# Feed-forward down projection: the short chunk of K moved from first to last, its first column half joined to the last seven-product passes

## The chip, the cores and the metric

The kernel runs on one core of one Trainium2 chip, in one launch. The metric is device time in microseconds (us): a median of three runs. The engines are named as the profile names them: PE (TensorE) multiplies, DVE (VectorE) and ACT (ScalarE) work elementwise, POOL (GpSimd) and SP (SyncE) mostly issue transfers.

## What is computed

The reference is a two-layer encoder on 256 positions with 2048 channels, all in 32-bit floats. Each layer has a mixer (attention with pooling in layer 0, an mLSTM in layer 1) and then a gated MLP. The change touches the MLP alone:

```python
def conv_ffn(x, w_up, conv_w, conv_b, w_down):
    u = x @ w_up
    up = jnp.pad(u, ((0, 0), (1, 1), (0, 0)))
    c = conv_w.astype(u.dtype)
    u = c[0] * up[:, :-2] + c[1] * up[:, 1:-1] + c[2] * up[:, 2:] + conv_b.astype(u.dtype)
    gate, val = jnp.split(u, 2, axis=-1)
    return (jax.nn.silu(gate) * val) @ w_down
```

`w_up` is 2048 x 11264 and `w_down` 5632 x 2048. The layer's output is the residual `x` plus this; it feeds the next RMS norm, or, after layer 1, is the result.

## The kernel before, in words

**Split weights.** Every weight is streamed in chunks of 128 x 1024 floats. `Stream.load` (L105) has SP load a chunk into one of 7 buffers `w`; `Stream.split` (L126) has ACT round it to a high part (L137) and DVE subtract that to get the low part (L138), both into one of 4 buffers `hl`. A product then takes three matmuls: high by high, high by low, low by high. With four `hl` buffers, the split of a chunk can only begin once PE is done with the chunk four before it. The number in a name such as `hl382` is the chunk's place in the whole stream.

**The MLP.** `ffn_layer` works through a list of steps that `_ffn_plan` writes. An `up` step (L1110) makes one 128-wide tile of the 5632 hidden channels: 64 matmuls over 4 weight chunks, then a copy by ACT (L441), adds by DVE (L442, L1114), the convolution (ACT L1119 to L1121, DVE L1122 and L1123), the SiLU gate (L1127, L1128) and the split into the tile `g` (L1129, L1130). There are 44 of them. The down projection sums over these 44 tiles; they are taken in chunks of K, `FCH = [4, 8, 8, 8, 8, 8]`, and its work is woven in behind the `up` steps.

**Seven products in place of eight.** For a pair of K tiles and one half of the columns (two blocks of 512), the plain way takes eight 128 x 128 x 512 products. The kernel takes seven, in two kinds of pass: A makes four (PSUM tiles 4, 6, 5, 3) and B three (0, 1, 2). A step such as `A1` is a pass of kind A on column half 1. Within a pass, steps of one unit handle two pairs: 24 matmuls over 4 weight chunks for A, 18 over 3 for B. A needs sums of the `g` tiles (`combine`, L1132: tiles `sf`, then `s3`, `s1`) and sums of weights. The latter are made by transfers into DRAM far ahead (`premix`, L478: the tiles `m`), or, for every other pair, by a load with an accumulating transfer from POOL (`sum`, L123) and two adds by DVE on the next chunk (L133, L134).

**Draining.** The PSUM pool `ps` has four tiles. When a pass ends, `drain` (L1187, adds at L1199) moves its three or four tiles into `acc` and `x`, one DVE add each. After the last pass of a column half, `total` (L1209) does the eight adds (L1216) that combine the products into the four quarters of `x` in that half. PE executes in the order of the code; DVE, ACT, POOL and SP stand in an order that a scheduler sets.

**The end of the list before.** The last chunk of K has half of its pairs taken with seven products on column half 1 only (`A1+`, `B1+`); everything else of it goes the plain way. Passes of chunk 4 run as `A0 A1 A1+ B0 B1 B1+`. Behind the last `up` step stand two units of B1, the plain block 0 in part (`down_two`, L1266), the unit B1+, the rest of the plain blocks 0 and 1, and then half of the K tiles of blocks 2 and 3 (`down`, L1250). In layer 1 the very last block is `down_end` (L1222), which finishes in three pieces. In layer 0, `Norm.add` (L315) starts on each finished block: squares on ACT, transposes on PE (`xt`, L326) and the split into `xx` (ACT L338, DVE L341), which the mLSTM's first matmuls (`mv`) read.

Of the kernel before, what the change touches and what calls it, by code (L numbers as in the profile page):

```python
# [9 lines left out]
F32 = mybir.dt.float32  # L10
# [6 lines left out]
P = 128  # L17
# [14 lines left out]
FT = DFF // P  # L32
FCH = [4, 8, 8, 8, 8, 8]
CH = 8
BOTH = ((0, 1, 2, 3, 4), (0, 1, 2, 3, 4))
LAST = (4, 4)

PASSES = (
    ("A1 B1 A0 B0", "A1 B1 A0 B0", "A1 B1 A0 B0", "A1 B1 A0 B0", "A0 A1 A1+ B0 B1 B1+"),
    ("A1 B1 A0 B0", "A1 B1 A0 B0", "A1 B1 A0 B0", "A1 B1 A0 B0", "A0 A1 A1+ B0 B1 B1+"),  # L40
)
# [178 lines left out]
def trunk(ctx: ExitStack, tc: tile.TileContext, gx, xT, xn, call, catt, cml, weights, mixes, out):  # L220
# [869 lines left out]
    def ffn_layer(layer, norm, nxt):  # L1090
        with ExitStack() as es:
# [7 lines left out]
            combos, pss, quads, seen, twos = {}, {}, {}, set(), []  # L1099
# [109 lines left out]
            def total(h):  # L1209
# [5 lines left out]
                for n, (to, op, e) in enumerate(steps):  # L1215
                    tc.keep_in_program_order(op(to, to, e))  # L1216
# [33 lines left out]
            def down(c, b):  # L1250
                gt, last = gts[c], c == len(FCH) - 1
                kts = list(range(_direct(layer, c, b), FCH[c]))
# [8 lines left out]
                if last and nxt is None:  # L1261
                    nc.sync.dma_start(out[:, :, b * 512 : b * 512 + 512], x[:, :, b * 512 : b * 512 + 512])
                elif last:
                    nxt.add(b)

            def down_two(c, second):  # L1266

                gt, n = gts[c], FCH[c]
                if not second:
                    twos.extend(mmp.tile([P, 2, 512], F32, tag="mm", name=f"dn{layer}_{c}_{b}") for b in range(2))  # L1270
                parts = [(ps, kts) for kts in (range(n - 2), range(n - 2, n)) for ps in twos]
                for ps, kts in parts[1:] if second else parts[:1]:
                    mov_part(ps, lambda k: gt[:, k], list(kts), kts[0] == 0, kts[-1] == n - 1)
                if not second:
                    return
                wv.until(lambda: ("A", 0) not in seen or ("total", 0) in pss)
                for b, ps in enumerate(twos):
                    residual(ps, b)
                    if nxt is None:
                        nc.sync.dma_start(out[:, :, b * 512 : b * 512 + 512], x[:, :, b * 512 : b * 512 + 512])  # L1280
                    else:
                        nxt.add(b)
# [3 lines left out]
            for kind, c, i, *j in _ffn_plan(layer):  # L1286
                if kind == "up":
# [4 lines left out]
                    if layer == 0 and (c, i) == (len(FCH) - 2, 5):  # L1292
                        premix(2, 25.0, 25.0, 0)
                elif kind == "down":
                    down(c, i)
                elif kind == "two":
                    down_two(c, i)
# [96 lines left out]
def _halves(layer, c):  # L1394

    return () if c == len(FCH) - 1 else (0, 1) if c in BOTH[layer] else (1,)


def _pairs(layer, c):

    return (LAST[layer] if c == len(FCH) - 1 else FCH[c]) // 2


def _direct(layer, c, b):

    return LAST[layer] if c == len(FCH) - 1 and b >= NB // 2 else 0


def _ffn_plan(layer):

    slots, late, units = [[] for _ in range(FT)], [], []
    at = 1
    for c in range(len(FCH) - 1):
        at = max(at + (c == 0) * FCH[0], sum(FCH[: c + 1]))
        step = len(_halves(layer, c))
        for pas in PASSES[layer][c].split():  # L1420
# [191 lines left out]
```

## Time and profile before

| what | before |
|---|---|
| median of 3 runs | 2147.94 us (2147.16 to 2148.05) |
| span of the profiled execution | 2145.3 us, so 2.6 us of the median lie around it |
| busy: PE, DVE, ACT, POOL | 100%, 83%, 67%, 13% of the span |
| DMA | 606.66 MB, mean 283 GB/s |
| last `up` of layer 0, of layer 1 (start) | 905.85 us, 2085.44 us |

A row of a timeline or group gives the start, the busy time, the engine, the line, the operation, what is written and read, and how often; in brackets or behind a bar stands how long the engine was idle before it and what ended that. Busy matmuls overlap: the time that a run of them takes is read from the start of one row to the start of the next.

### The profile page before, as it was taken

The page shows a single profiled execution, that of the slowest core. Times are in us where ns is not written, and L with a number is a line of the kernel's source. Part 1 is how long each engine was busy: PE and PEld are TensorE (multiplying, and loading weights), DVE is VectorE, ACT ScalarE, POOL GpSimd, SP SyncE. Part 2 cuts the span into 40 slices and gives each one's busy share as a digit, 9 for nine tenths or more (in the row PEclk, how much of TensorE's full clock was granted, in tenths as well). Part 3 has the DMA queues.
Part 4 walks back from the last instruction along what each step waited for, and adds up shares of the span by engine and source line. Part 5 has one row for each costly group of instructions (what it writes and reads, how often), then busy time and mean ns, then how long its engine had stood idle before and what let it go on. Part 6 is the DMA issues. An engine that isn't in the chain of part 4 may idle for free.

```text
span 2145.3 us, 32359 instructions
## 1 busy us (share of the span) xinstructions
PE 2139.5 (100%) x11364; PEld 1834.6 (86%) x11364; DVE 1784.1 (83%) x2524; ACT 1444.6 (67%) x2199; POOL 287.6 (13%) x366
## 2 busy tenths in 40 slices
PE   9999999999999999999999999999999999999999
PEld 7888888888888888889888888888888888888887
DVE  7786678889988899898878786567888899889988
ACT  6665577777777767766556564557776777777774
POOL 0022112111111111111111111111111111100000
PEclk9999999999999999999999999999999999999999
DMA  9678889899999999998889798988999999888875
GB/s 333 210 213 256 262 248 317 275 327 329 318 331 320 321 300 306 307 296 237 276 276 299 232 308 236 280 242 247 313 291 333 337 311 317 288 259 266 255 249 189
DMA packets 181543, 606.66 MB, mean 283 GB/s; under 512 B 23707, under 2 KB 26563, under 8 KB 181379
## 3 DMA queue, kind: packets, MB, share of 16 engines
q1 hardware_dynamic: 133952, 478.60, 62.4%
q0 software_dynamic: 28384, 70.54, 19.4%
q10 hardware_dynamic: 19042, 55.45, 7.8%
q8 instruction: 89, 1.46, 0.3%
q14 instruction: 76, 0.61, 0.1%
HBM read 602.35 MB, written 104.90 MB: 330 GB/s over the span
## 4 chain that ended last, share of the span: by engine, by line
PE 97%; DVE 2%; issue 1%; DMA 0%; ACT 0%; ACTq 0%; DVEq 0%
PE up L275 45%; PE pp L275 16%; PE op L275 8%; PE mq L275 4%; PE mk L275 4%; PE mo L275 3%; PE mv L275 3%; PE qproj L275 3%; PE dn L275 3%; PE mp L275 1%; PE kproj L275 1%; PE vproj L275 1%; DVE hl L138 1%; PE pool L275 1%; PE av L275 1%
## 5 line engine op out<-in xcount | busy, mean ns | idle before, releaser
L138 DVE TENSOR_TENSOR hl<-w,hl 128x1024 fp32r<-128x1024 f32 (+1 forms) x869 | 1048.0, 1217 | 179.1 <-ACT hl L137 172.1
L137 ACT CAST hl<-w 128x1024 fp32r<-128x1024 f32 (+1 forms) x868 | 891.2, 1046 | 384.8 <-PE up L275 118.3
L275 PE MATMUL up<-xx,hl 128*128 128x512 f32 (+1 forms) x5632 | 993.6, 337 | 0.0
L275 PEld LDWEIGHTS up<-xx,hl 128*128 128x128 f32 x5632 | 867.0, 188 | 130.0
L491 POOL DMA_DIRECT2D m<-m x184 | 147.4, 816 | 942.9 <-PE up L275 414.0
L275 PE MATMUL pp<-hl,s 128*128 128x512 f32 x912 | 226.5, 390 | 0.4
L275 PEld LDWEIGHTS pp<-hl,s 128*128 128x128 f32 x912 | 168.1, 188 | 34.4 <-DVE hl L138 1.6
L275 PE MATMUL pp<-hl,g 128*128 128x512 f32 x684 | 173.9, 390 | 0.0
L275 PEld LDWEIGHTS pp<-hl,g 128*128 128x128 f32 x684 | 125.8, 188 | 24.4
L441 ACT COPY tb_up<-up 128x512 f32<-128x512 f32 x88 | 51.6, 587 | 116.5 <-PE up L275 116.5
L1122 DVE TENSOR_TENSOR y<-y,z 128x510 f32<-128x510 f32 x88 | 60.8, 690 | 63.2 <-ACT y L1121 62.7
L1121 ACT ACTIVATE y<-tb_up,conv 128x256 f32<-128x256 f32 x176 | 103.7, 589 | 0.0
L491 POOL DMA_DIRECT2D m<-in_dn x80 | 69.2, 864 | 247.1 <-PE up L275 59.4
L275 PE MATMUL mk<-xx,hl 128*128 128x512 f32 (+1 forms) x512 | 93.0, 338 | 0.0
L275 PE MATMUL mq<-xx,hl 128*128 128x512 f32 (+1 forms) x512 | 92.0, 337 | 0.0
L442 DVE TENSOR_TENSOR tb_up<-up,tb_up 128x512 f32<-128x512 f32 x88 | 60.9, 692 | 36.9 <-ACT tb_up L441 36.5
L275 PE MATMUL op<-hl,cat 128*128 128x512 f32 x384 | 91.5, 393 | 0.0
L1119 ACT ACTIVATE z<-tb_up,conv 128x256 f32<-128x256 f32 x176 | 88.2, 501 | 3.9 <-DVE tb_up L1114 2.0
L275 PE MATMUL op<-hl,mcat 128*128 128x512 f32 x384 | 89.7, 392 | 0.0
L275 PEld LDWEIGHTS mq<-xx,hl 128*128 128x128 f32 x512 | 79.2, 188 | 11.6
L275 PEld LDWEIGHTS mk<-xx,hl 128*128 128x128 f32 x512 | 79.3, 188 | 11.4
L1120 ACT ACTIVATE z<-tb_up,conv 128x256 f32<-128x256 f32 x176 | 87.4, 496 | 0.0
(256 smaller groups left out, 2178.8 us busy)
## 6 DMA issues: line engine op xcount, KB each, us to landing
w<-in_up SPq DMA_DIRECT2D x352, 512.0 KB, 6.6
w<-in_dn SPq DMA_DIRECT2D x174, 512.0 KB, 6.0
w<-in_m_in SPq DMA_DIRECT2D x118, 512.0 KB, 6.0
w<-m SPq DMA_DIRECT2D x98, 512.0 KB, 5.7
m<-in_dn ACTq DMA_DIRECT2D x160, 256.0 KB, 5.8
m<-m POOLq DMA_DIRECT2D x184, 128.0 KB, 6.0
w<-in_a_in SPq DMA_DIRECT2D x45, 512.0 KB, 5.5
m<-in_dn POOLq DMA_DIRECT2D x80, 256.0 KB, 7.2
```

Of the source, the lines that this page charges most:

```text
L137: (self.nc.vector.tensor_copy if i + c == 0 else self.nc.scalar.copy)(hl[:, 0, c : c + n], w[:, c : c + n])
L138: low = self.nc.vector.tensor_sub(hl[:, 1, c : c + n], w[:, c : c + n], hl[:, 0, c : c + n].bitcast(F32))
L275: last_mm[0] = pe.matmul(out_, lhsT, rhs, start=start, stop=stop, skip_group_check=True)
L441: a.copy(tb, ps[:, :, 1, :])
L442: v.tensor_add(tb, ps[:, :, 0, :], tb)
L491: paced(eng.dma_start(to[p : p + P // 2], src[p : p + P // 2], **kw))
L1119: a.activation(z[:, 0, j, :], u[:, j, :], AF.Copy, scale=cw(tl, 0))
L1120: a.activation(z[:, 1, j, :], u[:, j, :], AF.Copy, scale=cw(tl, 2))
L1121: a.activation(y[:, j, :], u[:, j, :], AF.Identity, scale=cw(tl, 1), bias=cw(tl, 3))
L1122: v.tensor_add(y[:, :, 1:S], y[:, :, 1:S], z[:, 0, :, 0 : S - 1])
```

## The change

`FCH` becomes `[8, 8, 8, 8, 8, 4]`: the short chunk is the last. All five full chunks take seven products on both halves, and of the last chunk column half 0 joins the last A0 and B0 passes (`A0+`, `B0+`); only blocks 2 and 3 of it go the plain way, four K tiles each. The last passes run as `A1 B1 A0 A0+ B0 B0+`. Since a pass begins when its chunk of `g` is there, six units now stand behind the last `up` step and the one B1 unit after it. `down_two` is gone; `finished` stores a block or hands it to the norm, for blocks 0 and 1 once `total(0)` is through.

```diff
-FCH = [4, 8, 8, 8, 8, 8]
+FCH = [8, 8, 8, 8, 8, 4]
...
-    ("A1 B1 A0 B0", "A1 B1 A0 B0", "A1 B1 A0 B0", "A1 B1 A0 B0", "A0 A1 A1+ B0 B1 B1+"),
...
+PASSES = ("A1 B1 A0 B0",) * 4 + ("A1 B1 A0 A0+ B0 B0+",)
...
-                    if h == 0 or n % 2:
+                    if h == 1 or n % 2:
                         yield 1.3
                 pss["total", h] = True
+                if h == 0:
+                    for b in range(2):
+                        finished(b)
+                        yield 0.6
+                    pss["half"] = True
+
+            def finished(b):
+
+                if nxt is None:
+                    nc.sync.dma_start(out[:, :, b * 512 : b * 512 + 512], x[:, :, b * 512 : b * 512 + 512])
+                else:
+                    nxt.add(b)
...
-                if last and nxt is None and b == NB - 1:
+                if nxt is None and b == NB - 1:
+                    wv.until(lambda: "half" in pss)
                     down_end(gt, b, kts)
                     return
...
-                if last:
-                    wv.until(lambda: ("total", 1) in pss)
+                wv.until(lambda: ("total", 1) in pss and (nxt is None or "half" in pss))
                 residual(ps, b)
...
-            def down_two(c, second):
...
-def _halves(layer, c):
-
-    return () if c == len(FCH) - 1 else (0, 1) if c in BOTH[layer] else (1,)
+def _halves(c):
+
+    return (0,) if c == len(FCH) - 1 else (0, 1)
...
-    seq += [("two", c, 0)] + [units[e] for e in late] + [("two", c, 1)]
-    return seq + [("down", c, b) for b in range(2, NB)]
+    for n, u in enumerate(late):
+        seq += [u] + after.pop(FT + n, [])
+    return seq + [("down", len(FCH) - 1, b) for b in range(NB) if b // 2 not in _halves(len(FCH) - 1)]
```

In the whole program PE has 24 matmuls fewer (192 fewer into `dn`, 168 more into `pp`). DVE and ACT split 12 chunks more each; DVE has 8 more adds into `w`, 20 more small ones in `combine`, and 8 fewer of `dn` into `x`. POOL and ACT issue 24 and 16 more transfers for `m`, SP and POOL 4 more each for `sum`.

The first place is PE behind the last `up` of layer 0; `pp0_4_10` to `pp0_4_12` are the tiles of B1, `pp0_4_03` to `pp0_4_06` those of A0, `dn0_5_0` is block 0 taken the plain way. Before:

```order
L275 MATMUL pp0_4_12_9016<-hl382_9019,s10_4_0_7333 128x512 x3
L275 MATMUL pp0_4_12_9016<-hl382_9019,s10_4_1_7343 128x512 x3
L275 MATMUL pp0_4_10_9014<-hl383_9031,g0_4_6558 128x512 x3
L275 MATMUL pp0_4_11_9015<-hl383_9031,g0_4_6558 128x512 x3
L275 MATMUL pp0_4_10_9014<-hl384_9043,g0_4_6558 128x512 x3
L275 MATMUL pp0_4_11_9015<-hl384_9043,g0_4_6558 128x512 x3
L275 MATMUL pp0_4_12_9016<-hl385_9056,s10_4_2_7503 128x512 x3
L275 MATMUL pp0_4_12_9016<-hl385_9056,s10_4_3_7804 128x512 x3
L275 MATMUL dn0_5_0_9090<-hl386_9068,g0_5_7809 128x512 x12
L275 MATMUL dn0_5_0_9090<-hl387_9080,g0_5_7809 128x512 x12
L275 MATMUL dn0_5_0_9090<-hl388_9094,g0_5_7809 128x512 x12
```

And now, at the same place:

```order
L269 MATMUL pp0_4_10_8868<-hl379_8955,g0_4_7172 128x512 x3
L269 MATMUL pp0_4_11_8869<-hl379_8955,g0_4_7172 128x512 x3
L269 MATMUL pp0_4_10_8868<-hl380_8974,g0_4_7172 128x512 x3
L269 MATMUL pp0_4_11_8869<-hl380_8974,g0_4_7172 128x512 x3
L269 MATMUL pp0_4_12_8870<-hl381_9018,s10_4_2_8128 128x512 x3
L269 MATMUL pp0_4_12_8870<-hl381_9018,s10_4_3_8430 128x512 x3
L269 MATMUL pp0_4_04_9052<-hl382_9029,s30_4_0_7953 128x512 x3
L269 MATMUL pp0_4_06_9053<-hl382_9029,s30_4_0_7953 128x512 x3
L269 MATMUL pp0_4_05_9054<-hl383_9040,s30_4_0_7953 128x512 x3
L269 MATMUL pp0_4_03_9055<-hl383_9040,g0_4_7172 128x512 x3
L269 MATMUL pp0_4_04_9052<-hl384_9056,s30_4_1_7963 128x512 x3
L269 MATMUL pp0_4_06_9053<-hl384_9056,s30_4_1_7963 128x512 x3
```

Where plain products on `dn` followed, with 12 matmuls to a weight chunk, the next pass now follows at once, with 6 matmuls to a chunk. In the unit `A0+` further on, the matmuls on `hl392` read `s30_5_1`, the sum made of the last `up` step's tile.

The second place is DVE at the time when the last `up` step's tile `g0_5` is finished. Before:

```order
L138 TENSOR_TENSOR hl390_9130<-w390_9066,hl390_9130 128x1024
L138 TENSOR_TENSOR hl391_9147<-w391_9078,hl391_9147 128x1024
L1128 TENSOR_TENSOR s0_42_8863<-s0_42_8863,y0_43_9000 128x256
L138 TENSOR_TENSOR hl392_9158<-w392_9092,hl392_9158 128x1024
L1130 TENSOR_TENSOR g0_5_7809<-s0_42_8863,g0_5_7809 128x256
L138 TENSOR_TENSOR hl393_9169<-w393_9110,hl393_9169 128x1024
L138 TENSOR_TENSOR hl394_9181<-w394_9128,hl394_9181 128x1024
L1199 TENSOR_TENSOR acc0_2460<-acc0_2460,pp0_4_10_9014 128x512
L138 TENSOR_TENSOR hl395_9199<-w395_9145,hl395_9199 128x1024
```

And now:

```order
L1124 TENSOR_TENSOR g0_5_8435<-s0_42_8863,g0_5_8435 128x256
L1210 TENSOR_TENSOR x_91<-x_91,acc0_2460 128x512 x2
L1131 TENSOR_TENSOR sf0_5_1_9116<-sf0_5_1_9116,s0_42_8863 128x128
L132 TENSOR_TENSOR hl392_9178<-w392_9126,hl392_9178 128x1024
L132 TENSOR_TENSOR hl393_9190<-w393_9138,hl393_9190 128x1024
L132 TENSOR_TENSOR hl394_9201<-w394_9152,hl394_9201 128x1024
L1210 TENSOR_TENSOR x_91<-x_91,acc0_2460 128x512
L1132 TENSOR_TENSOR sf0_5_1_9116<-sf0_5_1_9116,s0_42_8863 128x128
L132 TENSOR_TENSOR hl395_9214<-w395_9164,hl395_9214 128x1024
L1137 TENSOR_TENSOR s30_5_1_9120<-sf0_5_1_9116,s30_5_1_9120 128x384
```

The low part of `s30_5_1` stands behind the split of `hl395` and behind all eight adds of `total(1)` (L1210, the former L1216).

The third place is the end of DVE's list in layer 1. Before:

```order
L1216 TENSOR_TENSOR x_91<-x_91,acc1_13827 128x512 x2
L451 TENSOR_TENSOR x_91<-x_91,dn1_5_2_20564 128x512 x2
L1216 TENSOR_TENSOR x_91<-x_91,acc1_13827 128x512
L1247 TENSOR_TENSOR x_91<-x_91,end0_20604 128x512
L1247 TENSOR_TENSOR x_91<-x_91,end1_20605 128x256
L1247 TENSOR_TENSOR x_91<-x_91,end2_20606 128x256
```

And now:

```order
L1210 TENSOR_TENSOR x_91<-x_91,acc1_13887 128x512 x3
L1210 TENSOR_TENSOR acc1_13887<-acc1_13887 128x512
L1253 TENSOR_TENSOR x_91<-x_91,end0_20724 128x512
L1253 TENSOR_TENSOR x_91<-x_91,end1_20725 128x256
L1210 TENSOR_TENSOR x_91<-x_91,acc1_13887 128x512 x2
L1253 TENSOR_TENSOR x_91<-x_91,end2_20726 128x256
L1210 TENSOR_TENSOR x_91<-x_91,acc1_13887 128x512
```

The last add of the program was one on the `end` tiles; it is now the last of `total(0)`, which finishes block 1, and SP issues the store of block 1 last.

More of the change, by code (lines that the diff above doesn't have):

```diff
@@ L1257, in down @@
                 mov_part(ps, lambda k: gt[:, k], kts, True, True)
-                if last:
-                    wv.until(lambda: ("total", 1) in pss)
+                wv.until(lambda: ("total", 1) in pss and (nxt is None or "half" in pss))
                 residual(ps, b)
[L1261 to L1264, printed above, removed]
-            def down_two(c, second):
[L1268 to L1282, printed above, removed]
+                finished(b)
             wv.add(norm.finish(), 4.0)
             f, gts = 0, []
-            for kind, c, i, *j in _ffn_plan(layer):
+            for kind, c, i, *j in _ffn_plan():
                 if kind == "up":
@@ L1486, in _ffn_weights @@
             u += 4
-        elif kind in ("down", "two"):
-            n = FCH[c] // 2 - 1
-            out += [next(down) for _ in range((n, n + 2)[i] if kind == "two" else (FCH[c] - _direct(layer, c, i)) // 2)]
+        elif kind == "down":
+            out += [next(down) for _ in range(FCH[c] // 2)]
         elif kind != "mix":
@@ L1596, in ffn @@
     def ffn(l):
-        out, m = _ffn_weights(l, chunks(f"up{l}"), [chunks(f"dn{l}{j}") for j in range(11)])
+        out, m = _ffn_weights(chunks(f"up{l}"), [chunks(f"dn{l}{j}") for j in range(11)])
         mixes.append(m)
```

78 lines of the change are left out of this document (26 added, 52 removed).

## The prediction

> **What bounds the kernel now.** I read the page first, then the waits of PE, then the chain of waits, and then the timelines of PE and DVE around the last `up` step of a layer, where the change is made. The page's head, its busy times and its chain:
>
> ```profile
> span 2145.3 us, 32359 instructions
> PE 2139.5 (100%) x11364; PEld 1834.6 (86%) x11364; DVE 1784.1 (83%) x2524; ACT 1444.6 (67%) x2199; POOL 287.6 (13%) x366
> ...
> PE 97%; DVE 2%; issue 1%; DMA 0%; ACT 0%; ACTq 0%; DVEq 0%
> ```
>
> PE is the bound nearly everywhere, and fewer matmuls are worth their full time wherever PE stays fed. DVE, at 83%, is next. The view of waits on PE alone lists all that PE waited for:
>
> ```profile
> PE wps L299 <- DVE pad L707: 1.2, 1, 1.2
> PE mo L275 <- DVE tb_k L442: 0.7, 1, 0.7
> PE atr L907 <- DVE A L901: 0.3, 1, 0.3
> ```
>
> The question is whether PE stays fed in the one stretch that is rewritten. The timeline of PE at the end of layer 1's MLP before (start, busy time):
>
> ```profile
> 2081.35 2.89 PE L275 MATMUL pp<-hl,g 128*128 128x512 f32 x12
> 2084.08 1.52 PE L275 MATMUL pp<-hl,s 128*128 128x512 f32 x6
> 2085.44 11.30 PE L275 MATMUL up<-xx,hl 128*128 128x512 f32 x64
> 2096.58 2.89 PE L275 MATMUL pp<-hl,g 128*128 128x512 f32 x12
> 2099.31 1.52 PE L275 MATMUL pp<-hl,s 128*128 128x512 f32 x6
> 2100.67 2.88 PE L275 MATMUL pp<-hl,g 128*128 128x512 f32 x12
> 2103.39 1.93 PE L275 MATMUL pp<-hl,s 128*128 128x512 f32 x6
> 2105.15 8.33 PE L275 MATMUL dn<-hl,g 128*128 128x512 f32 x36
> ```
>
> The last `up` takes 2096.58 - 2085.44 = 11.14 us, a B unit 4.09. Six `pp` matmuls take 1.52 us, but at 2103.39 they take 1.93: with only two B units behind the last `up`, PE already loses 0.41 us to DVE. Then `dn` comes to its relief: 36 matmuls on three weight chunks, 2.7 us for each chunk, where a `pp` unit uses one up every 1.36 us (4.09 / 3).
>
> **PE's work.** An A unit has its row in the chain of waits:
>
> ```profile
> 1999.94 5.45 PE pp L275 x24
> ```
>
> So a matmul is 227 ns, and the 24 that go are worth 5.45 us. The two losses of 0.41 go with the old order, about -0.8 in both layers. The passes in the steady part of a layer, one unit behind each `up`, keep their form; I cost those at nothing, since no wait of PE stands there now. If that cover were gone, it would be by DVE's share of a longer list, which is the next term.
>
> **DVE behind the last `up`, once in each layer.** How far apart DVE's instructions begin when nothing holds them is read from full stretches of its timeline, in layer 1 and in layer 0:
>
> ```profile
> 2072.76 3.49 DVE L138 TENSOR_TENSOR hl<-w,hl 128x1024 fp32r<-128x1024 f32 x3
> ...
> 2082.17 0.69 DVE L442 TENSOR_TENSOR tb_up<-up,tb_up 128x512 f32<-128x512 f32 x1 [1.06 <-ACT tb_up L441]
> ...
> 2104.89 1.29 DVE L1216 TENSOR_TENSOR x<-x,acc 128x512 f32<-128x512 f32 x2
> ```
>
> ```profile
> 836.43 0.42 DVE L1136 TENSOR_TENSOR sf<-s 128x256 f32<-128x256 f32 x1
> 836.77 0.42 DVE L1130 TENSOR_TENSOR g<-s,g 128x256 fp32r<-128x256 f32 x1
> ...
> 838.84 0.28 DVE L1137 TENSOR_TENSOR sf<-sf,s 128x128 f32<-128x128 f32 x1
> 839.04 2.35 DVE L138 TENSOR_TENSOR hl<-w,hl 128x1024 fp32r<-128x1024 f32 x2
> ...
> 843.25 0.55 DVE L1143 TENSOR_TENSOR s<-sf,s 128x384 fp32r<-128x384 f32 x1
> 843.72 2.36 DVE L138 TENSOR_TENSOR hl<-w,hl 128x1024 fp32r<-128x1024 f32 x2
> ```
>
> A split takes 1.14 us (3.49 for three less 2.35 for two), an add over 512 columns 0.60 (1.29 for two less 0.69 for one), one over 256 0.34 (836.43 to 836.77), over 128 0.20, over 384 0.47.
>
> Set the clock to 0 at the start of the last `up`. PE, if fed, ends it at 11.1, the B1 unit at 15.2, the two A0 units of chunk 4 at 26.1, and after the first pair of `A0+` (2.7) asks at 28.9 for `s30_5_1`, the sum over the tile that this very `up` made. Before, the last such sum was over tiles that were complete four `up` steps earlier, and the last tile itself was read by plain products alone, some 20 us after its `up` (two B units, three chunks of `dn` and the unit `B1+` lay between).
>
> DVE cannot run ahead. The split of `hl382`, the first of A0, needs the buffer that PE frees when the `up` ends; and DVE's order puts the `up`'s own first add ahead of it, which came 0.82 us after the end of an `up` (2082.17, against 2081.35, when PE passed on to `pp`). So DVE starts at 12.0, waits about 0.5 for ACT's half of `hl382` (a cast of 1.05 us that begins at 11.9, behind ACT's copy for the same `up`), and then executes in order, up to the low part of `s30_5_1`: 14 splits (`hl382` to `hl395`), 16.0 us; 17 adds over 512 columns (the `up` 4, the drain of B1 3, `total(1)` 8, weights 2), 10.2; three over 256, 1.0; two over 128, 0.4; two over 384, 0.9. That is 28.5 us, so `s30_5_1` is there at 12.0 + 0.5 + 28.5 = 41.0. PE asked at 28.9: **12.1 us late in each layer, 24.2 in both**. PE has by then also been slowed step by step (at `hl386`, `hl387` and so on, about 2 us to a chunk that it uses up in 1.36), and the last piece, from about 35 to 41, is one wait for `s30_5_1`.
>
> Nothing gives it back: the seven units from the last `up` on need 24 chunks in 32.7 us of PE. What follows, B0 and `B0+`, takes nine chunks in 12.3 us; DVE needs 9 x 1.14 + 4 x 0.60 = 12.7, two of the nine being split by then, so I add nothing there. ACT is not the bound: its cast has a mean of 1046 ns,
>
> ```profile
> L137 ACT CAST hl<-w 128x1024 fp32r<-128x1024 f32 (+1 forms) x868 | 891.2, 1046 | 384.8 <-PE up L275 118.3
> ```
>
> so 14 casts take 14.6 us of the same 28.5, and where DVE is full ACT has room (the window below: 12.56 us of 16.90). The handover of PSUM tiles between passes (B1 to A0 without an `up` between) costs up to 1.7 us by itself: A0's fourth tile waits for the third drain of B1, which DVE reaches at 18.9 by the same count, and PE asks at 17.3; it lies inside the 12.1. Bounds for this term: 9 us in each layer, if the late sum were ready when its splits are (the last 3 us less), and 14, if each step between DVE and PE adds its signals.
>
> **Transfers.** The queues get 12 weight chunks, 4 `sum` pairs and 40 `m` transfers more. In layer 0's tail the window row (PE, PEld, DVE, ACT, POOL busy, granted clock, DMA share, GB/s) is
>
> ```profile
> 916.98:933.88 16.90, 16.79 (x75) 13.60 (x74) 16.90 (x21) 12.56 (x17) 1.56 (x2) 1.00 0.99 307
> ```
>
> The transfers are full there, at 307 GB/s, and DVE too (16.90 of 16.90). At the slowed pace some 19 chunks of 0.52 MB have to come in 44 us, 225 GB/s, which leaves 80 of the 307 for `m`; so I take 0, at most 5 us in layer 0, where the share is already 0.99. In layer 1 no `m` is made at that time. POOL and SP carry the added `sum` and `m` issues well ahead.
>
> **From layer 0 into the mLSTM.** Before, 84 `dn` matmuls lay between the last seven-product unit and the transposes, now 48 (10.9 us). The groups of DVE's splits there, and PE's timeline:
>
> ```profile
> L341 DVE SCALAR_TENSOR_TENSOR xx<-xt,gcol,xx 128x256 fp32r<-128x256 f32 x48 | 22.2, 479 | 5.3 <-ACT xx L338 5.0
> ...
> L138 DVE TENSOR_TENSOR hl<-w,hl 128x864 fp32r<-128x864 f32 x5 | 5.2, 1047 | 0.0
> ```
>
> ```profile
> 937.80 19.21 PE L275 MATMUL dn<-hl,g 128*128 128x512 f32 x84
> 956.85 1.91 PE L326 MATMUL xt<-cst,x 128*128 128x128 f32 x16
> ...
> 964.87 4.21 PE L275 MATMUL mv<-hl,xx 128*128 128x288 f32 x30
> ```
>
> In that time DVE has to do the drain of B0, `total(0)`, both plain blocks and the splits of the next weights. By its order, until block 1 is complete: 15 adds over 512 columns of drain, `total` and blocks, 9.0; splits of `hl406` to `hl409`, 1.14 + 3 x 0.97 (0.08 off each duration, as with the others, for the overlap); two of `xx`, 0.8; that is 13.9, and it begins 0.8 after the B0 unit, so it ends at 14.7. PE reaches the transposes of block 1 at 11.6 (10.9 and eight transposes): **+3.0**, once. The lower end is 0, if ACT's and DVE's orders leave the transposes of block 0 to fill it; the upper 7, if the same wait comes back at later K tiles.
>
> **The end of layer 1.** The last rows of PE, DVE and the stores:
>
> ```profile
> 2136.44 5.78 PE L275 MATMUL end<-hl,g 128*128 128x512 f32 x36
> ```
>
> ```profile
> 2142.25 0.42 DVE L1247 TENSOR_TENSOR x<-x,end 128x256 f32<-128x256 f32 x1 [0.30 <-PE end L275]
> ```
>
> ```profile
> out<-x SPq DMA_DIRECT2D x3, 512.0 KB, 4.4
> ...
> out<-x ACTq DMA_DIRECT2D x1, 128.0 KB, 1.7
> ```
>
> The span ends 3.1 us after the last matmul. Now `total(0)` still has three adds over 512 columns left when the `end` tiles are done, so DVE ends about 2.1 us after PE, not 0.4, and the last store is one of 512 KB (4.4) and not of 128 KB (1.7). 1.7 + 2.7 would be 4.4; the store shares its engines with little, so I take **+3.5** (2 to 4.5).
>
> **Sum**, against the profiled execution: 2145.3 - 5.45 - 0.8 + 24.2 + 3.0 + 3.5 = 2169.8. The median of the runs is 2.6 above the span; with it, 2172.4. I say 2172.
>
> **The rivals.** (1) *PE stays fed and only the matmuls count.* Then 2147.9 - 6.2 = 2141.7, faster. For it: PE is 100% busy and DVE has hidden everything so far. It decides at the rate of the splits: PE asks for a chunk every 1.36 us, and DVE would have to need less than that for a split with all that stands between. With 28.5 us for 14 it needs 2.0; the 0.41 us lost at 2103.39 says that there is no slack. (2) *Only the handover binds*: DVE's other adds are absorbed before the late sum is asked for, and there remain 1.7 us in each layer, the 3.0 and the 3.5: 2147.9 - 6.2 + 3.4 + 6.5 = 2151.6. Against it stands the fixed order, eight adds of `total(1)` between the splits. (3) *PE comes back slower after its long wait.* The profile's first matmuls, behind an idle PE, against the same shape in the middle:
>
> ```profile
> L299 PE MATMUL wps<-x 128*128 128x256 f32 x10 | 4.5, 641 | 1.2 <-DVE pad L707 1.2
> ...
> L275 PE MATMUL npr<-dg 128*128 128x256 f32 x4 | 1.2, 379 | 0.0
> ```
>
> They took 1.7 times as long. If the 18 matmuls behind the wait of about 6 us do the same, that is 18 x 0.227 x 0.7 = 2.9 us in each layer: 2178. [...] (4) *Transfers fall behind too*: the 5 us above and the upper ends of the other terms, 2172 + 5 + 4 = 2181.
>
> **How the numbers follow.** My forecast has 0.62; rival 3 has 0.18, rival 4 0.08, rival 2 0.07, rival 1 0.05. The range must hold the forecast with its bounds and rival 3. Low: 9 instead of 12.1 in each layer, 0 and 2 for the other terms is 2172 - 6.2 - 3 - 1.5 = 2161. High: rival 3 and the upper end of the end of layer 1 and of the mLSTM term, 2178 + 5 = 2183. Faster or slower counts from 0.2%, 4.3 us, about what a measurement of this kernel can tell from no change. Faster is rival 1 alone; within 0.2% falls a part of rival 2, 0.03; the rest is slower.
>
> **What would show it.** In the changed kernel PE's waits would have rows on `pp` for DVE's `hl` and `s`, with the longest near 6 us, twice; the run of `pp` behind the last `up` would take about 45 us where it was 33 by PE's rate. DVE would be without idle for some 28 us there. At the start of the mLSTM a wait of `xt` or `mv` for DVE of about 3 us; in layer 1 the last DVE row would be L1210 and the last transfer a store of 512 KB. It would be wrong if PE's row of `pp` stood unbroken at 227 ns a matmul, or if PE waited for DMA there.

## The result, and the profile after

| | before | after |
|---|---|---|
| median, this comparison | 2147.55 us (2146.99 to 2148.05, 4 runs) | 2194.62 us (2188.06 to 2196.51, 4 runs) |
| profiled execution: span, its own time | 2145.3, 2147.94 | 2192.7, 2194.73 |

The ratio is 1.0215, with a 95% interval of 1.02 to 1.0229: 47 us slower. The direction was forecast, the size was not: 2194.6 lies outside 2161 to 2183, and the loss is about twice the forecast 24. The head of the page and the chain of waits after:

```profile
span 2192.7 us, 32488 instructions
PE 2152.1 (98%) x11340; PEld 1835.3 (84%) x11340; DVE 1802.6 (82%) x2556; ACT 1459.1 (67%) x2219; POOL 312.9 (14%) x394
...
PE 88%; DVE 5%; DMA 4%; issue 1%; ACT 1%; ACTq 0%; DVEq 0%; SPq 0%
```

The 24 matmuls are gone, yet PE is busy 12.6 us longer and the span is 47.4 us longer. DVE is no busier as a share (82%, before 83%), and still it ended the waits: an average over the span hides a stretch of 30 us in which it is full. PE's waits after (engine, line, who it waited for; us in total, times, longest):

```profile
PE pp L269 <- DVE hl L132: 8.7, 10, 3.8
PE pp L269 <- DVE s L1137: 7.2, 2, 3.6
PE xt L320 <- DVE x L1210: 5.1, 3, 3.0
PE pp L269 <- ACT s L1136: 3.1, 2, 1.5
PE cols L269 <- ACT rows_b L827: 2.9, 1, 2.9
```

Before, the whole list came to 2.2 us. To see where the 47.4 us lie, the span is cut at four places of PE's timeline: the start of the last `up` of layer 0, the mLSTM's first `mq`, the first `up` of layer 1 and the last one. The kernels of the experiments stand in the same table (us, from the profiled execution of each):

| kernel | to the last `up`, layer 0 | to `mq` | to layer 1 | to its last `up` | to the end |
|---|---|---|---|---|---|
| before | 905.9 | 84.4 | 445.9 | 649.3 | 59.9 |
| after | 906.6 | 108.7 | 453.8 | 648.5 | 75.1 |
| e1_mix_sooner | 904.4 | 107.4 | 451.8 | 648.0 | 76.1 |
| e2_no_total1 | 907.4 | 101.7 | 453.5 | 648.0 | 67.2 |
| e3_fill | 909.0 | 106.1 | 447.2 | 648.0 | 73.5 |
| e4_plain_between | 904.5 | 106.9 | 452.8 | 648.0 | 71.3 |
| e5_total1_late | 909.4 | 103.3 | 447.3 | 648.0 | 70.5 |
| e6_total1_pool | 909.0 | 108.8 | 452.1 | 648.0 | 75.1 |
| e7_no_m | 905.2 | 101.0 | 445.4 | 648.0 | 75.6 |
| e8_late_sooner | 903.9 | 98.3 | 451.4 | 648.0 | 70.5 |
| e9_no_total0_l0 | 907.9 | 105.6 | 446.5 | 648.0 | 75.2 |
| e10_shift_alone | 904.6 | 100.5 | 448.3 | 648.0 | 74.2 |
| e11_shift_late_sooner | 903.9 | 101.5 | 445.7 | 648.0 | 74.2 |

From before to after that is +0.8, +24.3, +7.9, -0.8 and +15.2. The last column is the clean one: its transfers are not full (the window of that stretch shows a share of 0.65), and kernels that are alike there agree within 1 us (after, e1, e7, e9: 75.1 to 76.1). The first column moves between 904.5 and 909.4 among e2 to e6 and e9, whose edits concern only what stands behind that place. The third moves between 445 and 454; why is said under **Open** below, and no verdict rests on it.

**Layer 1, where the forecast can be checked alone.** PE's timeline from its last `up`:

```profile
2117.57 11.30 PE L269 MATMUL up<-xx,hl 128*128 128x512 f32 x64
...
2143.30 0.73 PE L269 MATMUL pp<-hl,s 128*128 128x512 f32 x2 [1.16 <-DVE hl L132]
...
2154.14 0.73 PE L269 MATMUL pp<-hl,s 128*128 128x512 f32 x2 [1.55 <-ACT s L1136]
2158.47 3.35 PE L269 MATMUL pp<-hl,s 128*128 128x512 f32 x7 [3.60 <-DVE s L1137]
2161.63 3.71 PE L269 MATMUL pp<-hl,g 128*128 128x512 f32 x15
2165.18 1.52 PE L269 MATMUL pp<-hl,s 128*128 128x512 f32 x6
...
2174.70 5.60 PE L269 MATMUL dn<-hl,g 128*128 128x512 f32 x24
```

The matmuls on the late sum begin at 2158.47, 40.9 us after the `up`; the forecast had 41.0. The stretch up to `dn` takes 57.13 us where its matmuls alone need 43.85 (11.14 for the `up`, 4.09 for B1, 28.6 for 126 matmuls of 0.227): 13.3 lost, forecast 12.1. DVE's list between, its first and its last row:

```profile
2129.87 0.69 DVE L436 TENSOR_TENSOR tb_up<-up,tb_up 128x512 f32<-128x512 f32 x1
...
2157.87 0.75 DVE L1137 TENSOR_TENSOR s<-sf,s 128x384 fp32r<-128x384 f32 x2
```

No row between them shows an idle time: DVE runs through, 28.6 us from 2129.87 to the end of the longer of the two, 2158.4 (28.5 forecast).

**The clock.** Windows of 2 us of the same stretch (window; PE, PEld, DVE, ACT and POOL busy; granted clock, DMA share, GB/s):

```profile
2152.00:2154.00 2.00, 0.59 (x3) 0.17 (x1) 2.00 (x4) 1.67 (x3) 0.00 (x0) 1.00 0.86 254
2154.00:2156.00 2.00, 0.73 (x2) 0.30 (x2) 2.00 (x3) 0.09 (x1) 0.00 (x0) 0.75 0.79 223
2156.00:2158.00 2.00, 0.00 (x0) 0.00 (x0) 2.00 (x5) 0.30 (x1) 0.00 (x0) 0.50 0.90 342
2158.00:2160.00 2.00, 1.53 (x4) 1.24 (x5) 1.31 (x3) 0.00 (x0) 0.00 (x0) 0.50 0.93 322
2160.00:2162.00 2.00, 2.00 (x7) 1.57 (x6) 0.98 (x2) 1.04 (x1) 0.00 (x0) 0.54 0.66 262
2162.00:2164.00 2.00, 2.00 (x10) 1.65 (x9) 2.00 (x3) 1.05 (x1) 0.00 (x0) 1.00 0.13 16
```

In PE's second wait and behind it the granted clock is 0.50, for some 6.8 us in all, and is 1.00 again some 3.3 us after the matmuls came back; seven of them take 3.35 us. In windows of 0.5 us it is 1.00 up to 2155.0 and 0.51 in the next, 0.66 from 2161.5 and 1.00 from 2162.0. Ahead of that PE had stood still for 1.55 us, then been busy for 0.73 with two matmuls, and stood still again from 2154.87 on. Rival 3 came true beside the forecast.

**The end.** The last DVE row is an add of `total(0)`, at 2187.74, as forecast, and the span ends 6.8 us after the last matmul, before 3.1: +3.7, forecast 3.5.

**Layer 0** loses more. A wait of PE for a split, DVE's row that holds that split up, and the transfer behind it in the chain of waits (issue, us to landing):

```profile
925.97 1.04 PE L269 MATMUL pp<-hl,s 128*128 128x512 f32 x2 [3.75 <-DVE hl L132]
```

```profile
922.77 0.69 DVE L127 TENSOR_TENSOR w<-w,sum 128x512 f32<-128x512 f32 x1 [3.48 <-DMA w<-in_dn]
```

```profile
909.26 13.41 DMA w<-in_dn
...
1020.72 6.53 DMA gd<-gr
```

A weight chunk took 13.4 us to arrive. It was no exception: of the weight loads from `in_dn` issued between 880 and 906 us the middle one took 11.4 us (6 loads), before 6.9 (7 loads). The windows over the 125 us ahead of the last `up`, before and then after, show why transfers matter here:

```profile
780.00:905.85 125.85, 125.85 (x673) 108.04 (x672) 111.04 (x143) 91.08 (x139) 13.68 (x18) 1.00 0.94 302
```

```profile
780.00:906.61 126.61, 125.31 (x665) 106.32 (x663) 111.99 (x148) 88.68 (x132) 24.11 (x30) 1.00 1.02 328
```

302 GB/s have become 328, the share 1.02: full. Further on PE waits at the entrance to the mLSTM and in it:

```profile
981.24 0.90 PE L320 MATMUL xt<-cst,x 128*128 128x128 f32 x3 [3.04 <-DVE x L1210]
...
988.36 0.55 PE L320 MATMUL xt<-cst,x 128*128 128x128 f32 x3 [1.87 <-DVE x L1210]
...
1029.42 1.07 PE L269 MATMUL cols<-cst,rows_b 40*128 40x40 f32 x4 [2.91 <-ACT rows_b L827]
```

The last goes back to the small transfer `gd` of the chain above: 6.53 us for 40 KB.

### The profile page after: what moved, and what is told of

It is laid out like the page before. It is cut to its first block, busy times and chain, and to the rows that moved or that the text cites. A ratio compares the mean times of both kernels' runs of the same rounds, so it can differ in the third digit from the quotient of the medians.

```text
span 2192.7 us, 32488 instructions
## 1 busy us (share of the span) xinstructions
PE 2152.1 (98%) x11340; PEld 1835.3 (84%) x11340; DVE 1802.6 (82%) x2556; ACT 1459.1 (67%) x2219; POOL 312.9 (14%) x394
## 4 chain that ended last, share of the span: by engine, by line
PE 88%; DVE 5%; DMA 4%; issue 1%; ACT 1%; ACTq 0%; DVEq 0%; SPq 0%
PE up L269 42%; PE pp L269 15%; PE op L269 8%; PE mk L269 4%; PE mq L269 4%; PE qproj L269 3%; PE mv L269 3%; PE mo L269 3%; DVE hl L132 3%; DMA w<-in_dn 2%; PE mp L269 1%; PE vproj L269 1%; PE kproj L269 1%; PE pool L269 1%; DVE x L1210 1%
## 5 line engine op out<-in xcount | busy, mean ns | idle before, releaser
L132 DVE TENSOR_TENSOR hl<-w,hl 128x1024 fp32r<-128x1024 f32 (+2 forms) x877 | 1056.2, 1215 | 187.8 <-ACT hl L131 177.9
L131 ACT CAST hl<-w 128x1024 fp32r<-128x1024 f32 (+2 forms) x876 | 899.4, 1046 | 389.9 <-PE up L269 107.1
L485 POOL DMA_DIRECT2D m<-m x200 | 162.3, 828 | 965.5 <-PE up L269 424.0
L269 PE MATMUL pp<-hl,s 128*128 128x512 f32 x1008 | 259.3, 398 | 20.9 <-DVE hl L132 8.7
L269 PEld LDWEIGHTS pp<-hl,s 128*128 128x128 f32 x1008 | 188.0, 191 | 66.2 <-DVE hl L132 14.6
L269 PE MATMUL pp<-hl,g 128*128 128x512 f32 x756 | 193.4, 392 | 0.7 <-DVE x L1193 0.7
L269 PEld LDWEIGHTS pp<-hl,g 128*128 128x128 f32 x756 | 140.4, 189 | 28.8 <-DVE x L1193 1.1
L485 POOL DMA_DIRECT2D m<-in_dn x88 | 75.3, 856 | 292.3 <-PE up L269 61.2
```

What stands on the lines that cost most here:

```text
L131: (self.nc.vector.tensor_copy if i + c == 0 else self.nc.scalar.copy)(hl[:, 0, c : c + n], w[:, c : c + n])
L132: low = self.nc.vector.tensor_sub(hl[:, 1, c : c + n], w[:, c : c + n], hl[:, 0, c : c + n].bitcast(F32))
L269: last_mm[0] = pe.matmul(out_, lhsT, rhs, start=start, stop=stop, skip_group_check=True)
L485: paced(eng.dma_start(to[p : p + P // 2], src[p : p + P // 2], **kw))
```

## The experiments

The theory after the result has two parts: behind the last `up`, DVE's list sets PE's pace, with the halved clock on top; and in layer 0 the added `m` transfers hold up the weights. The rivals: DVE alone, transfers alone, or the one late sum alone. All edits are to the kernel after (2194.62), and each kernel was timed in rounds with the kernel before, which stood at 2147.1 to 2147.8.

### e1_mix_sooner: 2188.50 us, ratio 1.0191 (1.0176 to 1.0206)

```diff
-            premix(0, 26.0, 33.0, 8)
+            premix(0, 26.0, 28.0, 8)
```

> The kernel after takes 2194.6 us. Its layer 0 loses 2.1 us before the last up step, 18.85 behind it where layer 1 loses 13.3, and 2.9 at the mLSTM's cols, where a small transfer took 6.5 us. Here the schedule of premix gets the m tiles of layer 0 done some up steps earlier; nothing else differs. Theory: in layer 0 the transfers of m, with 328 GB/s and a DMA share of 1.02, hold up the weights, so the early stalls go from 2.1 to about 0, the stretch behind the last up from 18.85 to about 13.3, and the transfer before cols from 6.5 to about 3: 9 to 11 us in all, 2184. Rival: DVE's list explains layer 0 as well as layer 1, and the waits for DMA are only where it comes late: no change, 2194, within 2 us.

6.1 us less, more than the rival's 2, less than the theory's 9. The first column went from 906.6 to 904.4 and the wait for the late weight from 3.75 to 0.88; the wait of `cols` stayed (2.5). So the transfers cost something, and sooner `m` takes away only a part. This run alone does not prove it: the two kernels' intervals overlap, and e4, with the `m` of after, has a first column of 904.5 too. The pair e5 and e8 below, which differ in this one line, shows 7.0 us clear of the noise.

### e2_no_total1: 2177.77 us, ratio 1.0138 (1.0121 to 1.0155)

```diff
-                for n, (to, op, e) in enumerate(steps):
+                for n, (to, op, e) in enumerate(steps if h == 0 else []):
```

> The eight adds of total(1) are left out in both layers, so the products of column half 1 stay uncombined in the output; PE and the transfers have the same work as in the kernel after, 2194.6 us. Theory: DVE's list behind the last up step sets when the late sum is there, so eight adds of 0.60 us off it bring 4.8 us in each layer, 9.6 in all: 2185, with layer 1's stretch losing 8.5 us instead of 13.3. Rival: the wait is for weights that come late or for ACT, and DVE would only wait in the adds' place: no change, 2194, within 2 us.

16.9 us less, where 9.6 was expected. In layer 1, PE's wait for the sum:

```profile
2144.28 1.88 PE L269 MATMUL pp<-hl,s 128*128 128x512 f32 x7 [1.31 <-DVE s L1137]
```

That is 33.8 us after the last `up` began (2110.46), 7.1 sooner than in after. Eight adds are 4.8; the other 2.3 are two splits, for in DVE's row 12 of them stand ahead of the sum now and 14 did in after. The clock stays at 1.00 (a row of seven takes 1.88 us, not 3.35), which, less a new wait of 0.60 behind it, makes up the 7.9 of the last column. DVE's list ahead of the sum sets the time there; the wait for weights or ACT, the rival, would have stayed.

### e3_fill: 2185.31 us, ratio 1.0177 (1.0162 to 1.0192)

```diff
+                    if kind == "A" and c == len(FCH) - 1 and m == 4:
+                        fill = mmp.tile([P, 2, 512], F32, tag="mm", name=f"fill{layer}")
+                        for n in range(18):
+                            mm(fill[:, 0], gts[c - 1][:, 0, 0, :P], xx(0).rearrange("p a b -> p (a b)"), n == 0, n == 17)
```

> In each layer 18 matmuls of 227 ns into a spare PSUM tile stand on PE just ahead of the products that read the late sum, where PE waited 3.6 us and then ran at a granted clock of 0.50. Theory: the low clock comes from PE's idleness and costs about 1.8 us in each layer (22 matmuls at 0.45 instead of 0.23, of which DVE hides a part); the added 4.1 us of matmuls lie inside the wait and keep the clock up; total 2191, 3.6 less, with 36 matmuls more and a clock near 1.00 behind them in layer 1. Rival A: PE at half clock is waiting for DVE anyway, so the low clock costs nothing: 2194 to 2196. Rival B: the clock drop does not come from idleness: it stays at 0.50 and 2194 or more.

PE in layer 1, with the fill, and the clock in a window behind it:

```profile
2145.08 4.24 PE L269 MATMUL fill<-xx,g 128*128 128x512 f32 x18
...
2151.15 1.89 PE L269 MATMUL pp<-hl,s 128*128 128x512 f32 x7 [1.37 <-DVE s L1137]
2152.87 3.56 PE L269 MATMUL pp<-hl,g 128*128 128x512 f32 x15
2156.27 1.52 PE L269 MATMUL pp<-hl,s 128*128 128x512 f32 x6
```

```profile
2152.00:2154.00 2.00, 2.00 (x10) 1.64 (x9) 1.99 (x4) 1.26 (x2) 0.00 (x0) 1.00 0.94 328
```

The sum is there when it was before, 40.9 us after the `up` (2110.24), but the 22 matmuls behind it take 5.12 us (2151.15 to 2156.27) where after took 6.71 (2158.47 to 2165.18). In layer 0 they take 5.12 too, where after took 7.09. So 36 useless matmuls save 1.6 us in layer 1 and 2.0 in layer 0, about as expected (1.8), by keeping the clock up; both rivals fall. The whole gain is 9.3, more than that: the third column alone is 6.6 shorter, because ACT's order in the mLSTM came out differently (see **Open**).

### e4_plain_between: 2185.81 us, ratio 1.0186 (1.0170 to 1.0201)

```diff
+        seq += [({2: "down", 3: "add"}[n], len(FCH) - 1, b) for b in plain if n in (2, 3)]
```

(`down` without its adds, before the third late unit, `add` behind that unit. `down_end` falls away: the last block finishes in one piece.)

> The two plain blocks of each layer stand ahead of the unit A0+, so that 10.9 us of matmuls that need a weight chunk only every 2.7 us lie before the late sum is asked for; their adds come right behind that unit. The work is the same. Theory: what counts is DVE's whole list from the end of the last up, about 55 us where PE's is 44; the wait for the sum shrinks by about 11 us and comes back behind B0+, where total(0), the norm and the stores stand bare: total 2194, within 4 us. Rival: only the sum of the last up's own tile is late, and all else behind it would flow: about 8 to 11 us less in each layer, 2172 to 2178.

The wait for the late sum is gone altogether, and of the 15.2 us in the last column only 3.8 went: PE ends at 2173.31, and the span at 2183.5, 10.2 us later, with `total(0)` and the stores bare. In all 8.8 less, between the two expectations. The late sum is not what costs by itself, it is the place where a full DVE shows first; e10 below, which has no such sum, says the same.

### e5_total1_late: 2182.17 us, ratio 1.0164 (1.0147 to 1.0181)

```diff
+                if kind == "A" and h == 0 and (len(FCH) - 1, FCH[-1] // 2 - 1) in combos:
+                    pss["late"] = True
...
+                if h == 1:
+                    yield from wv.wait(lambda: "late" in pss)
```

> All the work is kept; the eight adds of total(1) begin only when A0+ has been written, so in DVE's order they stand behind the late sum, and with them out of the way two splits that are not needed before it stand behind it too (as without total(1), where the sum was there at 33.8 us after the last up began, not at 40.9). Theory: PE's loss is the lateness of that sum and the low clock behind it, and behind the sum DVE has idle time (2.6 us while PE works through B0, 2.2 at the plain blocks) that takes the adds: 5 to 8 us less in each layer, 2194.6 - 13 = 2181. Rival: DVE's whole list up to the end sets the time, the adds only change place, and what is won at the sum comes back behind it: 2190 to 2195, with only the clock's 1.6 us in each layer gained.

12.5 less, near the theory's 13. In layer 1 the sum comes at 33.8 us, as in e2, but behind it waits turn up that after did not have:

```profile
2141.83 1.90 PE L269 MATMUL pp<-hl,s 128*128 128x512 f32 x7 [1.31 <-DVE s L1137]
...
2146.70 2.36 PE L269 MATMUL pp<-hl,g 128*128 128x512 f32 x9 [0.77 <-DVE acc L1195]
2150.26 1.63 PE L269 MATMUL pp<-hl,s 128*128 128x512 f32 x6 [1.20 <-ACT hl L131]
```

Of the 8.7 us won (7.1 and the clock's 1.6), the last column keeps 4.6. That the total comes near 13 is in part luck: outside the third column, which is 6.5 shorter here (see **Open**), the profile is 7.7 us shorter than that of after. Moving work behind the bottleneck pays as far as there is idle time behind it.

### e6_total1_pool: 2196.00 us, ratio 1.0224 (1.0208 to 1.0239)

```diff
+                if h == 1:
+                    steps = [(to, {v.tensor_add: g.tensor_add, v.tensor_sub: g.tensor_sub}[op], e) for to, op, e in steps]
```

> The eight adds of total(1) are done by POOL, which stands idle at that time. On POOL an add over 256 columns took 1.2 us in the profile of after, so eight of 512 need some 19 us, from about 18 to 37 us behind the start of the last up, and x is wanted at 57. Theory: what counts is DVE's list alone, so this is worth what leaving the adds out is worth, 16.8 us: 2178, DVE's other durations unchanged. Rival: an add on POOL slows DVE's own work beside it, so that DVE's splits stretch beyond 1.22 us while POOL adds: 2185 to 2195.

No gain at all: the rival was right. POOL's adds, and DVE beside them and behind them:

```profile
2135.67 6.18 POOL L1212 TENSOR_TENSOR x<-x,acc 128x512 f32<-128x512 f32 x3
```

```profile
2136.70 0.68 DVE L1193 TENSOR_TENSOR x<-x,pp 128x512 f32<-128x512 f32 x1
2137.30 1.17 DVE L1116 TENSOR_TENSOR y<-y,z 128x510 f32<-128x510 f32 x1
2138.39 2.31 DVE L132 TENSOR_TENSOR hl<-w,hl 128x1024 fp32r<-128x1024 f32 x1
...
2150.56 1.21 DVE L132 TENSOR_TENSOR hl<-sum,hl 128x1024 fp32r<-128x1024 f32 x1
```

While POOL adds (to 2149), a split takes 2.31 us and not 1.21, an add of `y` 1.17 and 1.77 and not 0.68; the one add among them that reads an operand from PSUM (`pp`, at 2136.70) keeps its 0.68. What DVE was spared it lost again: its rows beside POOL's took 7.7 us longer in all, where the eight adds had taken 4.8.

### e7_no_m: 2177.78 us, ratio 1.0140 (1.0125 to 1.0155)

```diff
+        if layer != 1:
+            for s0, s1, r, made in mixes[layer]:
+                for e, src in zip(made, (s0, r)):
+                    e.ap = src
+            return
```

> The weights that transfers make ahead (the m tiles) for layer 0's MLP and for the mLSTM are left out: the loads read one of the plain weights in their place, so the output lacks those sums, and the loads, the splits and the matmuls stay the same in number and size. Theory: layer 0 loses more than layer 1 because the transfers of m hold up the weights: the stall before the last up goes from 2.1 to 0, the stretch behind it from 62.7 to about layer 1's 57.1, the entrance to the mLSTM from 7.6 to about 4.5, and the wait of cols goes with what follows it, 5: together 16, 2179. Rival: DVE's list and the norm account for layer 0, and only the waits that the profile names for a late weight go: 2.1 and about 3, 2189 to 2190.

16.8 less, near the theory's 16, not the rival's 5. The window of the stretch behind the last `up` of layer 0:

```profile
905.17:962.62 57.45, 48.34 (x210) 37.37 (x208) 52.43 (x66) 36.87 (x49) 0.00 (x0) 0.94 0.72 236
```

It takes 57.45 us, as layer 1's 57.13 does, where after took 62.70; PE does not wait at all from 780 to 905 in it. The DMA share of e7 from 780 to 905 us is 0.84 (265 GB/s; after 1.02), and over the whole run the loads of weights from `in_dn` take 4.8 us in the middle, where they took 7.3 in after. So without `m` layer 0 is layer 1 over again up to the mLSTM, and the `m` transfers, old and new together, are worth 9.1 us there (1.4 and 7.7 in the first two columns), while the kernel before hid its own. The other 8.4 of this profile lie in the third column, and they are not shown to be `m`'s: ACT's order came out differently here too (see **Open**). That the total is so near 16 is in part luck.

### e8_late_sooner: 2175.22 us, ratio 1.0127 (1.0112 to 1.0142)

The edits of e5 and e1 together.

> The late start of total(1) and the sooner m together, all work kept. If the two causes, DVE's list ahead of the late sum and the transfers of layer 0, are separate, the gains add up: 13 and 6, 2175. If both act through the same wait, the second brings little: 2180. In neither case does it reach the kernel before, 2147.5: the entrance to the mLSTM (7.6), the end (3.7) and what remains of the two sums' waits stand against 6.2 us of matmuls.

2175.2: the gain is 19.4 us, the two gains add up to 18.6, as the theory has it, and the rival's 2180 falls. The profiles do not bear out a sum so exact: outside the third column e8 saves 18.2 us, e5 7.7 and e1 3.1. So sooner `m` brings something on top of e5, but how far the two causes are separate stays open. It is the fastest version that keeps the change and all of its work, and 1.3% slower than the kernel before.

### e9_no_total0_l0: 2185.06 us, ratio 1.0168 (1.0153 to 1.0184)

```diff
-                for n, (to, op, e) in enumerate(steps):
+                for n, (to, op, e) in enumerate(steps if h or layer else []):
```

> The eight adds of total(0) are left out in layer 0 alone, so column half 0 of that layer stays uncombined in the output; layer 1 is as in the kernel after, 2194.6 us. Between the start of dn and the mLSTM's first full matmuls PE lost 7.6 us in layer 0, waiting for these adds on x. Theory: DVE's list sets the entrance, so eight adds of 0.60 off it bring 4.8 us and a loss of about 2.8 remains, from the norm's own steps: 2190. Rival: a weight chunk that came late (DVE stood 3.1 us there) and the norm's steps set the entrance: at most 1.5 us less, 2193 to 2195.

The entrance, from `dn` to the full run of `mv`, takes 23.3 us (969.36 to 992.62), in after 26.3 (969.31 to 995.61): 3.0 less, between the theory's 4.8 and the rival's 1.5. The first transposes no longer wait, a later one does, for the norm:

```profile
990.64 0.63 PE L320 MATMUL xt<-cst,x 128*128 128x128 f32 x4 [2.29 <-DVE rv_n L274]
...
992.62 13.70 PE L269 MATMUL mv<-hl,xx 128*128 128x288 f32 x96
```

The total fell by 9.6; the rest lies in the third column again (446.5 against 453.8), by ACT's order and not by the adds (see **Open**).

### e10_shift_alone: 2176.48 us, ratio 1.0130 (1.0115 to 1.0145)

```diff
-PASSES = ("A1 B1 A0 B0",) * 4 + ("A1 B1 A0 A0+ B0 B0+",)
+PASSES = ("A1 B1 A0 B0",) * 4 + ("A1 B1 A0 B0",)
...
-    return (0,) if c == len(FCH) - 1 else (0, 1)
+    return () if c == len(FCH) - 1 else (0, 1)
```

> The short chunk stays last, but joins no pass: all four blocks of it go the plain way (11352 matmuls, 12 more than in after and 12 fewer than before), and no sum is made of the last up's tile. Theory: what costs is the density of DVE work behind the last up. In A0, DVE needs 20.5 us for eight splits and the adds where PE needs 14.1 from the time it can begin: 6.4 late; B0 about 1; then plain blocks with a chunk every 2.7 us hide total(0) and the stores: 7.5 in each layer, some 3 for layer 0's transfers, less 2.7 for 12 matmuls and 0.8 for the old losses: 2147.5 + 14.5 = 2162. Rival A: the joined units and their late sum are all of the cause, the shift costs nothing: 2144 to 2146. Rival B: the shift of passes behind the last up is all of it: 2190.

2176.5: both rivals fall (2145, 2190), and so does the theory's 2162. The short chunk's place alone costs 29 of the 47 us; joining its half to the passes costs the other 18, while it saves 12 matmuls. In layer 1's last column, where nothing else disturbs, the place alone makes 14.3 of the 15.2 us, although no late sum is left in this kernel; of the 18, the profiles put 8.2 into layer 0's way to `mq`, 2.0 into the first column and 5.5 into the third. PE at the change from A0 to B0 in layer 1:

```profile
2136.11 0.92 PE L269 MATMUL pp<-hl,g 128*128 128x512 f32 x3 [3.66 <-DVE acc L1193]
2139.49 4.21 PE L269 MATMUL pp<-hl,g 128*128 128x512 f32 x9 [2.46 <-DVE acc L1193]
```

What I had costed at about 1 are two waits of 3.66 and 2.46 for the drain, which stands in DVE's list behind splits and `total(1)`, with the granted clock at 0.50 behind them (2137.5 to 2143.5; nine matmuls in 4.21). At the end the plain blocks hide `total(0)`: the span ends 3.2 us after PE, as before.

### e11_shift_late_sooner: 2178.05 us, ratio 1.0143 (1.0126 to 1.0160)

As e10, `total(1)` behind the last A0's drain, and the `premix` line of e1.

> As e10_shift_alone, and total(1) begins only when the last A0 pass has been drained, and the m tiles of layer 0 are made sooner; all work kept. Theory: the eight adds go under the plain blocks, where DVE has room, and take 4 us off A0's lateness in each layer; layer 0's transfers no longer count: 2162 - 8 - 3 = 2151, at best the same as the kernel before. Rival: A0 is bound by the split and its cast, not by the adds ahead of them: 2158 to 2162.

Neither 2151 nor 2160: nothing is gained over e10, and the last column is 74.2 us in both. The waits of e10 are smaller, and another has come in their place, PE on `dn` for the add of an earlier block, which DVE reaches late:

```profile
2155.86 8.53 PE L269 MATMUL dn<-hl,g 128*128 128x512 f32 x24 [5.88 <-DVE x L445]
```

DVE shows no idle time from 2111.97 until that add has ended at 2155.7, 44 us. Here the new order of DVE's list only chose where PE waits, while in e5 it had won 4.6 us of the same column.

## Why the prediction was right in direction and wrong in size

- **PE's work** (-5.45) **and the two old losses** (-0.8): as forecast; the matmul rows still stand at 227 ns.
- **DVE behind the last `up`** (12.1 in each layer): right in mechanism, in order and in size. The sum came after 40.9 us (41.0), DVE's list was 28.6 us (28.5), and layer 1's stretch lost 13.3; e2 and e5 show that the list is the cause. The 1.2 more lies within the clock's price. The late sum itself was not essential: e10 has none and loses 14.3 us of the 15.2 in the last column, mostly waiting for drains that stand in the same list.
- **The clock**, kept as rival 3 and not in the sum: it happened together with the forecast, not instead of it. Its price behind the late sum is 1.6 us in layer 1 and 2.0 in layer 0 (e3), forecast 2.9. The forecast's factor of 1.7 came from rows of the first 6 us of before, where the granted clock was 1.00, so before had shown no drop of the clock; behind the late sum seven matmuls took 3.35 us, in e3 1.89. The price was paid again behind other waits, in the third column (below).
- **The end of layer 1** (+3.5): 3.7, and gone in e10, where plain blocks cover `total(0)`.
- **Transfers: the step that failed.** "At the slowed pace some 19 chunks of 0.52 MB have to come in 44 us, 225 GB/s, which leaves 80 of the 307 for `m`; so I take 0, at most 5 us in layer 0, where the share is already 0.99." That was an average rate for a question of lateness. With the transfers full (1.02), a single chunk landed 13.4 us after its issue, and there are seven buffers; the average fits and the chunk is late. The runs put in its place 7.7 us: 2.1 before the last `up` of layer 0 (it starts 0.8 later, where six matmuls fewer ahead of it are worth 1.4; the first column scatters by more, 4.9) and 5.6 more behind it than in layer 1 (18.9 against 13.3, some of it the clock behind the 3.75 us wait). Both are gone in e7. The third column's 7.9 come on top.
- **Into the mLSTM** (+3.0, bounds 0 to 7): mis-sized. It lost 7.6 (26.3 us, of which the matmuls need 18.7). Without `total(0)` 4.6 remain (e9), without `m` 5.1 (e7: 962.62 to 986.41), so neither is all of it. DVE stood 3.1 us there behind a cast of ACT that waited 3.3 us for a weight, and the term had no row for that.

By terms: 24.5 forecast for the span; 2.1 + 5.6 + 2 x 1.2 + 4.6 + 7.9 + 0.2 more make 47.3, measured 47.4. Rival 4 had named the transfers' failing, but at 5 us, where the runs show 7.7 and a late small transfer in the third column besides; and the range held rival 3 or rival 4 alone, where both came. Rivals 1 and 2 are refuted: PE is not fed.

**Open**: the third column, +7.9 from before to after. What it is made of the traces show: PE's wait of 2.91 for `cols`, one of 1.0 further on, and the clock behind the first, 0.86 in the mean from 1025 to 1050, which is 3.5 us. The wait comes from ACT. In after it issues `G<-gd` (L868), the loads that need `gd`, ahead of the activation L827 on `rows_b` that PE waits for, and so it stands until `gd` has landed; in e9 the activation stands ahead. First after, then e9:

```profile
1020.72 0.55 ACTq L830 DMA_DIRECT2D gd<-gr  x1
1027.27 0.36 ACTq L868 DMA_DIRECT2D G<-gd  x1
1027.66 1.28 ACT L827 ACT_TABLE_LOAD   x1 [5.28 <-DMA gd<-gr]
```

```profile
1018.63 0.55 ACTq L830 DMA_DIRECT2D gd<-gr  x1
1019.22 1.28 ACT L827 ACT_TABLE_LOAD   x1 [2.19 <-DVE rows_b L826]
1025.95 1.67 ACTq L868 DMA_DIRECT2D G<-gd  x2
```

ACT's order is the scheduler's, and edits elsewhere changed it: before, e1, e2, e4 and e6 have that of after, the other seven that of e9, and none of these waits for `cols`. Before had the bad order too, but there `gd` landed 3.4 us after its issue and PE did not wait for `cols`, nor did it in e4; in after, e1, e2 and e6 it took 6.1 to 6.7. Two columns are long for another wait: e4 (4.1 us for `mvf`) and e8 (3.1 for a split). Why `gd` landed late in four kernels is not shown. That after itself has one run at 2188.06 among three at 2194.5 to 2196.5 would fit a `gd` that sometimes lands early; that is argued, not shown.

## What to carry to other kernels

Before work is moved to the end of a stage, count for each engine what must run between the last thing that comes in and the last that goes out: an engine at 82% of the span was full for 29 to 44 us just there, and no order that was tried there brought the kernel back to its time before. Cost a matmul saved against what feeds it: a product that uses up its weights twice as fast asks twice the splits in the same time. And where transfers are near full, ask how late a single one lands, not whether the average rate fits. Last, read an experiment's gain stretch by stretch: edits in the MLP changed ACT's order in the mLSTM, and 6 to 8 us that looked like their own gain came from there.

## What the runs showed of the hardware

- In layer 1 of after the granted clock fell to 0.50 where two matmuls lay between waits of 1.55 and 3.60 us: it was down from the first 0.5 us of the second wait and stayed down for 6.8 us. In layer 0, with waits of 1.55 and 3.58, it was down about 1 us into the second. In e3, where 18 matmuls filled the first wait and one of 1.37 us was left, it stayed at 1.00.
- In e6 an add over 512 columns on POOL took 1.3 to 2.1 us (6.18 for three), and DVE's split beside it up to 2.3 instead of 1.2, so that eight adds moved away from DVE (4.8 us) cost it 7.7.
- Between 880 and 906 us, weight loads of 0.52 MB from `in_dn` landed after 11.4 us in the middle where the DMA share was 1.02 (after) and after 6.9 at 0.98 (before). Over the whole run the middle one took 7.3 us in after, 6.0 in before and 4.8 in e7.
